# Differential attention: weights times values in three float32r passes for two query tiles at once

## The chip, the cores and the metric

The kernel runs on one core of one Trainium2 chip. The metric is the device time of one launch, in microseconds (us). Before the change three runs gave 2757.2 to 2759.38 us, with a median of 2757.73 us.

The engines are named as the profile names them: PE is TensorE's matrix multiplier, PEld its weight load, DVE is VectorE, ACT is ScalarE, POOL is GpSimd, SP issues the DMAs. A matmul has a *stationary* operand (the weights that are loaded) and a *moving* operand (what streams past it); its result lands in PSUM, which has eight banks of 512 fp32 numbers per partition.

## The reference, cut to what matters

The whole program is a two-layer encoder trunk: 1024 tokens, model width 1024, fp32. Layer 0 mixes tokens with neighbourhood attention, layer 1 with dense differential attention; each layer ends with a gated convolutional feed-forward part and a gated embedding. The change is in layer 1's attention, which has 8 heads, each with two score maps of width 64 and values of width 128:

```python
s = jnp.einsum('bhmqd,bhmkd->bhmqk', qb, k) + bias      # two maps m per head
a = jax.nn.softmax(s, axis=-1)
w = a[:, :, 0] - lam_full * a[:, :, 1]                  # one weight matrix
o = jnp.einsum('bhqk,bhkd->bhqd', w, v)                 # weights times values
o = rms_norm(o, subln_g) * (1.0 - lambda_init)          # norm over the 128 of a head
o = o.transpose(0, 2, 1, 3).reshape(B, S, D) @ w_o
```

## The kernel before, in words

**Order of the work.** The kernel is written in Python on top of a scheduler. TensorE's instructions run in exactly the order in which the program writes them (`manual_schedule` for PE). The order on ACT, DVE, POOL and SP is chosen when the program is compiled, by a planner that walks the program with estimated times; at run time every engine then works through its own list strictly in that order. Waits between engines are put in by the framework, from which part of a buffer each instruction reads or writes. A buffer out of a pool can be handed on only when the last reader of its previous content is done.

**Precision.** A product in fp32 is made in one of two ways. Either the fp32 operands go to a matmul as they are; such a 128x128x128 product shows as two PE instructions in the trace. Or both operands are split into a rounded part and a rest in the type float32r, `hi = round(x)` on ACT (`high`, L135) and `lo = x - hi` on DVE (`low`, L138), and three matmuls are made, hi*hi, hi*lo and lo*hi (`mm3`, L169 to L174).

**The stage of the change** is `da` (L659). It runs over 64 steps n, eight query tiles t of 128 for each of eight heads. For one n:

- `da_scores` (L583): twelve float32r matmuls make the two score maps of 128x1024 in four PSUM banks (pool "s", L598). Then `softmax_pre` per map: on DVE, add the bias and find the minimum (the scores carry a negative sign; L441); on ACT, the exponential with its sum (L445). Then on DVE the reciprocals (L605, L607), the factor (L606), and the combination of both maps into one weight matrix (L608). The row scale `r0` is kept for later.
- `da_turn` (L611), in two halves g: four 128x128 transposes on PE into one PSUM bank (L620), then a copy to `wT`: half 0 on ACT (L623), half 1 on DVE (L625).
- `da_values` (L627): eight fp32 products, with the turned weights `wT` stationary and the values `V` moving (L634). The result has queries on the partitions, so the head's norm is along the free axis: a square with sum on ACT (L637), a small DVE operation (L638), a power on POOL (L184), and the scaling on DVE (L640).
- `da_out` (L643): one transpose of the normed tile on PE (L648), a scaled copy on ACT (L653 or L656), a DMA to `oT` in HBM (L657).

`da` runs these one step apart: in iteration n it calls the values of n-1, the scores of n+1, the two halves of the turn of n, and the output of n-1.

**The stream.** Between them PE works on something else: `qkv_stream` (L296), a generator that makes the keys, queries and values of the *next* head, eight accumulating three-matmul steps per 512 columns. `tick(part)` (L403) takes `6 * part` steps from it. After a block the keys and queries are split out of PSUM (L135 with L138, L145 with L146); the values are copied (L382), turned by four transposes per half (`transposed`, L203), and copied on ACT to `v` (L372). `wblock` (L288) loads and splits the next weights. Near the end the stream goes on with the embeddings (`embeddings`, L1432) and the first rows of the output product (`first_out`, L782); their weights are split by `jobs`, one of which each call of `job` (L739) takes from a list and places behind two given instructions.

**PSUM.** The eight banks are four for the scores, two for the stream (pool "pj") and two in the pool "tr", which serves `bank()`: the values' result, the halves of the turn and the turned values. The values' bank is held from `da_values` to the copy in `da_out`, which reads it.

Of the kernel before, what the change touches and what calls it, by code (L numbers as in the profile page):

```python
# [16 lines left out]
P = 128  # L17
# [74 lines left out]
class Trunk:  # L92
# [203 lines left out]
    def qkv_stream(self, layer, hT, x, first, mid):  # L296
# [7 lines left out]
        for j in range(KT):  # L304
            A = self.page(self.r2, "r2", (P, 4, SEQ), F32R)
# [56 lines left out]
            if layer == 0:  # L362
                v = B[:, 2:4].rearrange("p a (t m w) -> p (a t) m w", t=4, m=2)

                def put(g, t):
                    o, t = v[:, 4 * g : 4 * g + 4], t.rearrange("p k (m w) -> p k m w", m=2)
                    self.split(t, o[:, :, :, 0:64], o[:, :, :, 64:128])
            else:
                v = self.page(x, "v", (P, KT, P))

                def put(g, t):
                    nc.scalar.activation(v[:, 4 * g : 4 * g + 4], t, AF.Copy)  # L372
# [64 lines left out]
    def softmax_pre(self, s, bias, e):  # L437

        nc = self.nc
        mn = self.col("mn")  # L440
        nc.vector.tensor_tensor_reduce(  # L441
            out=e, in0=s, in1=bias, scale=1.0, scalar=3e38, op0=ALU.add, op1=ALU.min, accum_out=mn
        )
        sm = self.col("sum")
        self.exp = nc.scalar.activation(e, e, AF.Exp, bias=mn, scale=-1.0, accum_out=sm).ins  # L445
        return sm
# [136 lines left out]
    def da_scores(self, x, n):  # L583
# [17 lines left out]
        r0, sm = [self.softmax_pre(s[m], self.T[:, a : a + SEQ], e[m]) for m in range(2)]  # L601
        w = e[0]
        self.chunk[n] = w, r0
# [7 lines left out]
    def da_turn(self, x, n, g):  # L611
        nc = self.nc
        w, r0 = self.chunk[n][:2]
        if g == 0:
            self.chunk[n] = w, r0, self.page(x, "wT", (P, KT, P))
        wT = self.chunk[n][2]
        t = self.bank()
        for k in range(4):
            c = (4 * g + k) * P
            nc.tensor.transpose(t[:, k * P : k * P + P], w[:, c : c + P], self.ident)  # L620
        t = t.rearrange("p (k t) -> p k t", k=4)
        if g == 0:
            self.turned_w = nc.scalar.activation(wT[:, 0:4], t, AF.Copy).ins  # L623
        else:
            self.job(self.turned_w, nc.vector.tensor_copy(wT[:, 4:8], t).ins)  # L625

    def da_values(self, x, n):  # L627
        nc = self.nc
        V = self.v[2 * (n // NT)]
        _, r0, wT = self.chunk[n]  # L630
        b = self.bank()
        o = b[:, :P]
        for k in range(KT):
            nc.tensor.matmul(o, wT[:, k], V[:, k], start=k == 0, stop=k == KT - 1)  # L634
        os = self.page(x, "os", (P, P))
        r = self.col("ss")
        nc.scalar.activation(os, o, AF.Square, scale=r0, accum_out=r)  # L637
        nc.vector.tensor_scalar(out=r, in0=r, scalar1=1.0 / P, scalar2=EPS, op0=ALU.mult, op1=ALU.add)  # L638
        self.root(r)
        nc.vector.tensor_scalar(out=os, in0=o, scalar1=r0, scalar2=r, op0=ALU.mult, op1=ALU.mult)  # L640
        self.chunk[n] = b, os

    def da_out(self, x, n, oT):  # L643
        nc = self.nc
        h, t = n // NT, n % NT
        b, os = self.chunk.pop(n)
        tr = b[:, P : 2 * P]
        nc.tensor.transpose(tr, os, self.ident)  # L648
        cols = slice(t * P, t * P + P)
        if h == D_HEADS - 1:  # L650
            if t == 0:
                self.opage = self.page(self.raw, "raw")
            nc.scalar.activation(self.opage[:, cols], tr, AF.Copy, scale=self.subg)  # L653
        else:
            ot = self.page(x, "ot", (P, P))
            nc.scalar.activation(ot, tr, AF.Copy, scale=self.subg)  # L656
            nc.sync.dma_start(oT[h][:, cols], ot)  # L657

    def da(self, hT, oT, first, mid):  # L659

        N = NT * D_HEADS
        with self.tc.tile_pool(name="xa1", bufs=2, reuse_waits="tile") as x, \
             self.psum("s", 2) as self.ps:
            self.begin(self.qkv_stream(1, hT, x, first, mid))
            self.chunk = {}
            self.need(self.qk, 0)
            self.tick(6 / 6)
            self.da_scores(x, 0)
            self.tick(6 / 6)
# [762 lines left out]
    def embeddings(self, layer):  # L1432

        nc = self.nc
        a = self.page(self.r2, "r2", (P, 2, 2, SEQ), F32R)
        b = self.page(self.r2, "r2", (P, 2, 2, D), F32R)
        load = []
        for k in range(2):
            rows = slice(k * P, k * P + P)
            for o, src in ((a, self.i["pT"]), (b, self.i["ple_w_proj"])):  # L1440
# [4 lines left out]
        else:  # L1445
# [16 lines left out]
            self.jobs += [job] * 4  # L1462
# [141 lines left out]
```

## Time and profile before

| | |
|---|---|
| median of three runs | 2757.73 us |
| the profiled execution's own time | 2757.19 us |
| its span, first to last instruction | 2755.4 us |
| mean granted TensorE clock | 0.994 |
| PE busy over the span | 98% |
| DVE, ACT, POOL busy over the span | 70%, 48%, 17% |
| the stage `da`, by the starts of its instructions | about 1348 to 1928 us |

Between the span and the execution's own time lie 1.8 us that the profile does not divide up. PE's ends are modelled, so that neighbouring matmuls overlap in the rows; what counts is the distance from one start to the next. A row of a timeline gives the start in us, the busy time in us, the engine, the line, the operation, the buffers, the shape and the count.

### The profile page before, as it was taken

The page shows a single profiled execution, that of the slowest core. Times are in us where ns is not written, and L with a number is a line of the kernel's source. Part 1 is how long each engine was busy: PE and PEld are TensorE (multiplying, and loading weights), DVE is VectorE, ACT ScalarE, POOL GpSimd, SP SyncE. Part 2 cuts the span into 40 slices and gives each one's busy share as a digit, 9 for nine tenths or more (in the row PEclk, how much of TensorE's full clock was granted, in tenths as well). Part 3 has the DMA queues.
Part 4 walks back from the last instruction along what each step waited for, and adds up shares of the span by engine and source line. Part 5 has one row for each costly group of instructions (what it writes and reads, how often), then busy time and mean ns, then how long its engine had stood idle before and what let it go on. Part 6 is the DMA issues. An engine that isn't in the chain of part 4 may idle for free.

```text
span 2755.4 us, 36831 instructions
## 1 busy us (share of the span) xinstructions
PE 2695.6 (98%) x13568; PEld 2229.1 (81%) x13568; DVE 1939.4 (70%) x3317; ACT 1320.1 (48%) x2467; POOL 463.2 (17%) x461
## 2 busy tenths in 40 slices
PE   7999998999999999999999999999999999999998
PEld 5888887877888888888788888887887888888887
DVE  5677777579777777676566666676688777776664
ACT  4555556354443445454355555555454434444452
POOL 2121120004333310001000000000105343300000
PEclk9999999999999999999999999999999999999999
DMA  6412214533332374343211111123413323372343
GB/s 183 172 53 68 63 52 151 147 92 110 113 105 90 115 263 129 101 151 109 99 46 46 45 46 46 54 77 120 141 61 122 115 92 115 97 285 96 115 143 106
DMA packets 129477, 298.49 MB, mean 108 GB/s; under 512 B 11753, under 2 KB 37737, under 8 KB 129297
## 3 DMA queue, kind: packets, MB, share of 16 engines
q1 hardware_dynamic: 129296, 296.15, 32.7%
q8 instruction: 106, 1.74, 0.3%
q14 instruction: 75, 0.61, 0.1%
HBM read 221.69 MB, written 86.61 MB: 112 GB/s over the span
## 4 chain that ended last, share of the span: by engine, by line
PE 86%; DMA 5%; DVE 5%; ACT 2%; issue 1%; POOL 0%; SPq 0%; ACTq 0%; POOLq 0%; DVEq 0%
PE b L172 20%; PE b L173 20%; PE b L174 20%; PE g L762 6%; PE m L762 5%; PE b L634 4%; PE s L598 3%; PE b L620 2%; PE b L203 2%; PE av L506 2%; PE b L488 1%; DMA r<-in_ffn_w_out 1%; PE b L762 1%; DMA raw<-in_qkv 1%; DMA x<-in_x 1%
## 5 line engine op out<-in xcount | busy, mean ns | idle before, releaser
L172 PE MATMUL b<-r,ws 128*128 128x512 f32 (+1 forms) x1328 | 550.1, 414 | 6.9 <-DVE u L1120 4.4
L173 PE MATMUL b<-r,ws 128*128 128x512 f32 (+1 forms) x1328 | 519.4, 391 | 1.0 <-DVE r L138 1.0
L174 PE MATMUL b<-r,ws 128*128 128x512 f32 (+1 forms) x1328 | 519.2, 391 | 0.5 <-DVE ws L138 0.5
L172 PEld LDWEIGHTS b<-r,ws 128*128 128x128 f32 x1328 | 253.0, 191 | 56.3 <-DVE u L1120 5.7
L174 PEld LDWEIGHTS b<-r,ws 128*128 128x128 f32 x1328 | 251.9, 190 | 54.7 <-DVE ws L138 1.0
L173 PEld LDWEIGHTS b<-r,ws 128*128 128x128 f32 x1328 | 253.7, 191 | 38.3 <-DVE r L138 3.1
L172 PE MATMUL b<-r,r 128*128 128x512 f32 x680 | 269.2, 396 | 8.5 <-ACT r L135 5.1
L184 POOL TENSOR_TENSOR ss<-ss,mhalf 128x1 f32<-128x1 f32 x136 | 84.3, 620 | 1136.8 <-DVE ss L638 564.5
L445 ACT ACTIVATE E<-E,mn 128x1024 f32<-128x1024 f32 (+2 forms) x256 | 221.4, 866 | 111.9 <-DVE mn L441 111.7
L172 PE MATMUL b<-r,wa 128*128 128x512 f32 x688 | 268.1, 390 | 3.2 <-DVE B L1132 2.9
L174 PE MATMUL b<-r,wa 128*128 128x512 f32 x688 | 268.0, 389 | 0.0
L173 PE MATMUL b<-r,wa 128*128 128x512 f32 x688 | 267.7, 389 | 0.0
L174 PE MATMUL b<-r,r 128*128 128x512 f32 x680 | 265.3, 390 | 1.0 <-DVE r L138 1.0
L173 PE MATMUL b<-r,r 128*128 128x512 f32 x680 | 265.7, 391 | 0.5 <-DVE r L138 0.5
L138 DVE TENSOR_TENSOR ws<-raw,ws 128x512 fp32r<-128x512 f32 (+3 forms) x168 | 171.7, 1029 | 59.8 <-ACT ws L135 57.2
L138 DVE TENSOR_TENSOR r<-raw,r 128x512 fp32r<-128x512 f32 (+1 forms) x170 | 129.1, 766 | 112.7 <-ACT r L135 109.6
L135 ACT ACTIVATE r<-raw 128x512 fp32r<-128x512 f32 (+1 forms) x170 | 112.4, 669 | 193.3 <-PE b L173 160.3
L135 ACT ACTIVATE ws<-raw 128x512 fp32r<-128x512 f32 (+3 forms) x168 | 124.2, 748 | 131.7 <-PE b L174 52.3
L172 PEld LDWEIGHTS b<-r,r 128*128 128x128 f32 x680 | 128.0, 188 | 37.4 <-ACT r L135 5.3
L762 PE MATMUL m<-r,ws 128*128 128x512 f32 x672 | 155.9, 391 | 0.0
L762 PE MATMUL g<-r,ws 128*128 128x512 f32 x672 | 155.8, 391 | 0.0
L172 PEld LDWEIGHTS b<-r,wa 128*128 128x128 f32 x688 | 129.1, 188 | 31.4 <-DVE B L1132 4.2
(178 smaller groups left out, 5144.1 us busy)
## 6 DMA issues: line engine op xcount, KB each, us to landing
raw<-in_w_in SPq DMA_DIRECT2D x86, 512.0 KB, 3.5
raw<-in_qkv SPq DMA_DIRECT2D x48, 512.0 KB, 5.6
spillS<-r SPq DMA_DIRECT2D x88, 256.0 KB, 3.2
r<-in_ffn_w_out SPq DMA_DIRECT2D x40, 512.0 KB, 10.5
raw<-spillS SPq DMA_DIRECT2D x40, 512.0 KB, 3.5
spillA<-B SPq DMA_DIRECT2D x66, 256.0 KB, 3.0
raw<-spillA SPq DMA_DIRECT2D x30, 512.0 KB, 3.9
x<-x SPq DMA_DIRECT2D x24, 512.0 KB, 3.5
```

Source lines behind the costliest of these rows:

```text
L135: return self.nc.scalar.activation(hi, src, AF.Copy).ins
L138: return self.nc.vector.tensor_tensor(out=lo, in0=src, in1=hi.bitcast(F32), op=ALU.subtract).ins
L172: mm(out, sta[0], mov[0], start=first, stop=False, skip_group_check=onto)
L173: mm(out, sta[0], mov[1], start=False, stop=False, skip_group_check=onto)
L174: mm(out, sta[1], mov[0], start=False, stop=last, skip_group_check=onto)
L184: self.nc.gpsimd.tensor_tensor(out=ss, in0=ss, in1=self.mhalf, op=ALU.pow)
L203: self.nc.tensor.transpose(t[:, k * P : k * P + P], h[:, c : c + P], self.ident)
L445: self.exp = nc.scalar.activation(e, e, AF.Exp, bias=mn, scale=-1.0, accum_out=sm).ins
L506: nc.tensor.matmul(out, V[:, kb, m], a[:, at * P : (at + w) * P], start=i + z == 0, stop=i == len(steps) - 1 and z == 1)
L598: nc.tensor.matmul(s[m][:, w], A[o, a, q], A[o, b, w], start=z == 0, stop=z == 2)
L634: nc.tensor.matmul(o, wT[:, k], V[:, k], start=k == 0, stop=k == KT - 1)
L762: mm(out[half], a, b[:, w], start=first and k + z == 0, stop=last and k == n - 1 and z == 2)
```

## The change

`da_values` now serves two query tiles at once, after every second tile. The roles are swapped: the values are stationary, split into hi and lo, and the turned weights of both tiles, also split, are the moving operand, 256 wide; each of the eight key blocks takes three matmuls (`mm3`). The result has the value's width on the partitions, so it is copied out on ACT and turned back by two transposes (`da_norm`) before the norm, and turned once more by `da_out`. Both halves of `da_turn` are now split (ACT and DVE) rather than copied, and so are the turned values. `wT` is one fixed buffer for a pair; it takes one of the four "r2" pages, and the heads' keys and queries go round the other three. The embeddings' operands move into those pages, their loads come in another order, and two of their four jobs are held back until the page they write is free. The ticks between the parts are new: half a tile's steps (0.5) between the halves of a turn, then 0.3 after an even-numbered tile and 0.7 after an odd-numbered one, ahead of the values.

```diff
@@ qkv_stream
-            A = self.page(self.r2, "r2", (P, 4, SEQ), F32R)
+            A = self.page(self.r2, "r2", (P, 4, SEQ), F32R) if layer == 0 else self.pages[j % 3]
...
-                v = self.page(x, "v", (P, KT, P))
+                v = self.page(x, "v", (P, 2, KT, P), F32R)
 
                 def put(g, t):
-                    nc.scalar.activation(v[:, 4 * g : 4 * g + 4], t, AF.Copy)
+                    self.split(t, v[:, 0, 4 * g : 4 * g + 4], v[:, 1, 4 * g : 4 * g + 4])
@@ da_turn
+        w, u = self.chunk[n], n % 2
         t = self.bank()
         for k in range(4):
             c = (4 * g + k) * P
-            nc.tensor.transpose(t[:, k * P : k * P + P], w[:, c : c + P], self.ident)
-        t = t.rearrange("p (k t) -> p k t", k=4)
-        if g == 0:
-            self.turned_w = nc.scalar.activation(wT[:, 0:4], t, AF.Copy).ins
-        else:
-            self.job(self.turned_w, nc.vector.tensor_copy(wT[:, 4:8], t).ins)
+            self.nc.tensor.transpose(t[:, k * P : k * P + P], w[:, c : c + P], self.ident)
+        did = self.split(t.rearrange("p (k t) -> p k t", k=4), *(a[:, 4 * g : 4 * g + 4, u] for a in self.wT))
+        if g == 1:
+            self.job(*did)
@@ da_values
-        o = b[:, :P]
+        o, (hi, lo) = b[:, : 2 * P], self.wT
         for k in range(KT):
-            nc.tensor.matmul(o, wT[:, k], V[:, k], start=k == 0, stop=k == KT - 1)
-        os = self.page(x, "os", (P, P))
...
+            self.mm3(
+                o, (V[:, 0, k], V[:, 1, k]), [a[:, k].rearrange("p u t -> p (u t)") for a in (hi, lo)], k == 0, k == KT - 1
+            )
+        os = self.page(x, "os", (P, 2, P), bufs=1)
+        self.nc.scalar.activation(os.rearrange("p u t -> p (u t)"), o, AF.Copy)
+        self.pair = b.rearrange("p (z u t) -> p z u t", z=2, u=2), os
+
+    def da_norm(self, x, n):
...
+        b, os = self.pair
+        r0 = self.sums.pop(0)
+        for u in range(2):
+            nc.tensor.transpose(b[:, 1, u], os[:, u], self.ident)
+        for u in range(2):
+            o, q, r = b[:, 1, u], r0[:, u : u + 1], self.col("ss")
+            nc.scalar.activation(os[:, u], o, AF.Square, scale=q, accum_out=r)
+            nc.vector.tensor_scalar(out=r, in0=r, scalar1=1.0 / P, scalar2=EPS, op0=ALU.mult, op1=ALU.add)
+            self.root(r)
+            nc.vector.tensor_scalar(out=os[:, u], in0=o, scalar1=q, scalar2=r, op0=ALU.mult, op1=ALU.mult)
@@ da_out
-        nc.tensor.transpose(tr, os, self.ident)
+        for u in range(2):
+            nc.tensor.transpose(b[:, 0, u], os[:, u], self.ident)
...
+        nc.scalar.activation(out, b[:, 0].rearrange("p u t -> p (u t)"), AF.Copy, scale=self.subg)
+        if h < D_HEADS - 1:
+            nc.sync.dma_start(oT[h][:, cols], out)
@@ da
+            self.pages = [self.page(self.r2, "r2", (P, 4, SEQ), F32R) for _ in range(4)]
+            w = self.pages[3].rearrange("p a n -> p (a n)").rearrange("p (z k u t) -> p z k u t", z=2, k=KT, u=2)
+            self.wT = w[:, 0], w[:, 1]
...
             for n in range(N + 1):
-                if n > 0:
+                if n % 2 == 0 and n > 0:
                     self.need(self.v, (n - 1) // NT * 2 + 1)
                     self.da_values(x, n - 1)
                 if n + 1 < N:
                     self.need(self.qk, (n + 1) // NT)
                     self.da_scores(x, n + 1)
+                if n + 1 >= N - NT - 1:
+                    self.jobs += self.after_keys
+                    self.after_keys.clear()
+                if n % 2 == 0 and n > 0:
+                    self.da_norm(x, n - 1)
+                elif n > 1:
+                    self.da_out(x, n - 2, oT)
                 if n < N:
                     self.da_turn(x, n, 0)
-                self.tick(0.34)
-                if n < N:
+                    self.tick(0.5)
                     self.da_turn(x, n, 1)
-                self.tick(0.16)
-                if n > 0:
-                    self.da_out(x, n - 1, oT)
-                self.tick(0.5)
+                    self.tick(0.7 if n % 2 else 0.3)
             self.drain()
+            self.da_out(x, N - 1, oT)
@@ embeddings
+            a, b = (self.pages[k].rearrange("p (k z) n -> p k z n", k=2) for k in (2, 0))
...
-            self.jobs += [job] * 4
+            self.jobs += [job] * 2
+            self.after_keys += [job] * 2
```

More of the change, by code (lines that the diff above doesn't have):

```diff
@@ L600, in da_scores @@
         e = [self.page(x, f"E{m}") for m in range(2)]
-        r0, sm = [self.softmax_pre(s[m], self.T[:, a : a + SEQ], e[m]) for m in range(2)]
-        w = e[0]
-        self.chunk[n] = w, r0
+        if n % 2 == 0:
+            self.sums.append(self.page(x, "r0", (P, 2)))
+        r0 = self.sums[-1][:, n % 2 : n % 2 + 1]
+        bias = self.T[:, a : a + SEQ]
+        self.softmax_pre(s[0], bias, e[0], r0)
+        sm = self.softmax_pre(s[1], bias, e[1])
+        w = self.chunk[n] = e[0]
         c = self.col("c")
@@ new lines, in da_turn @@
+        did = self.split(t.rearrange("p (k t) -> p k t", k=4), *(a[:, 4 * g : 4 * g + 4, u] for a in self.wT))
+        if g == 1:
+            self.job(*did)
+    def da_values(self, x, n):
+        V = self.v[2 * (n // NT)]
+        b = self.bank()
+        o, (hi, lo) = b[:, : 2 * P], self.wT
+        for k in range(KT):
+            self.mm3(
[4 more added lines that the diff above has]
+        self.pair = b.rearrange("p (z u t) -> p z u t", z=2, u=2), os
```

48 lines of the change are left out of this document (15 added, 33 removed).

## The prediction, made before the changed kernel had run

> **What bounds the kernel now.** I read the page first, then the stage in a table of windows, then PE's timeline, then DVE and ACT beside it.
>
> ```profile
> span 2755.4 us, 36831 instructions
> PE 2695.6 (98%) x13568; PEld 2229.1 (81%) x13568; DVE 1939.4 (70%) x3317; ACT 1320.1 (48%) x2467; POOL 463.2 (17%) x461
> ...
> PE 86%; DMA 5%; DVE 5%; ACT 2%; issue 1%; POOL 0%; SPq 0%; ACTq 0%; POOLq 0%; DVEq 0%
> ```
>
> ```profile
> 1435.00:1505.00 70.00, 70.00 (x448) 57.80 (x447) 47.09 (x96) 36.54 (x75) 4.40 (x8) 1.00 0.14 44
> ```
>
> PE carries 86% of the chain. In the second fence (length of the stretch, then PE, PEld, DVE, ACT, POOL busy, then the granted clock) one head of the stage fills PE without a gap at clock 1.00, with DVE busy 67% and ACT 52%. So a PE instruction removed here shortens the kernel, as long as DVE and ACT still keep up. One period, in PE's starts:
>
> ```profile
> 1444.15 1.95 PE L634 MATMUL b<-v,wT 128*128 128x128 f32 x16
> 1446.03 1.66 PE L598 MATMUL s<-r 64*128 64x512 f32 x12
> 1447.62 0.65 PE L620 MATMUL b<-ident,E 128*128 128x128 f32 x4
> 1449.50 0.60 PE L620 MATMUL b<-ident,E 128*128 128x128 f32 x4
> 1450.64 0.27 PE L648 MATMUL b<-ident,os 128*128 128x128 f32 x1
> 1452.82 1.95 PE L634 MATMUL b<-v,wT 128*128 128x128 f32 x16
> ```
>
> ```profile
> 1521.70 0.40 PE L172 MATMUL b<-r,ws 128*128 128x512 f32 x1
> ...
> 1522.39 0.39 PE L172 MATMUL b<-r,ws 128*128 128x512 f32 x1
> ```
>
> Start to start: values 1.88, scores 1.59, first half-turn to second 1.88, second to output 1.14, output to values 2.18; together 8.67 us a tile. A stream step is 0.69 (second fence). By the loop the three stretches hold 2, 1 and 3 steps, which leaves 0.50 and 0.45 for the half-turns and 0.11 for one transpose.
>
> **The change part by part.**
>
> *Values.* The new matmuls have 128x256 moving operands and weights that change as in `mm3`. The trace has that very form in the first projection:
>
> ```profile
> 18.14 0.41 PE L172 MATMUL b<-r,ws 128*128 128x256 f32 x1
> ...
> 20.06 0.41 PE L172 MATMUL b<-r,ws 128*128 128x256 f32 x1
> ...
> 24.09 0.28 PE L172 MATMUL b<-r,ws 128*128 128x256 f32 x1
> ...
> 26.49 0.28 PE L174 MATMUL b<-r,ws 128*128 128x256 f32 x1
> ```
>
> From 24.09 to 26.49 are 20 starts: 0.120 each. (From 18.14 to 20.06, while PE has just begun, nine starts: 0.213.) The stage runs at clock 1.00, so I take 0.120: 24 x 0.120 = 2.88 a pair, where two tiles cost 3.76. That saves 0.88.
>
> The Trainium skill ("TensorE: Matmul & The Clock Gate", Part 3, "The mechanism") speaks against this: a weight load overlaps running matmuls only if it goes to another row group. Here each load fills all rows, so load and stream would add up, and 24 loads would cost more than the page's count of instructions suggests. The rows at 0.120 do not agree: each holds a whole load.
>
> *Transposes.* One a tile (0.22 a pair) becomes two in the norm and two in the output, 4 x 0.11 = 0.44: +0.22.
>
> PE's work per pair falls by 0.66, from 17.34 to 16.68; 32 pairs: **-21.1 us**.
>
> *At the very end* there is no next score to cover the norm:
>
> ```profile
> PE b L648 <- DVE os L640: 1.9, 1, 1.9
> ```
>
> Afterwards the last norm waits only for the copy out of PSUM (about 0.2 handover and 0.4 copy, see below), and the stream's last steps cover the rest: 1.9 - 0.7 = **-1.2 us**.
>
> *DVE and ACT.* The copies become splits:
>
> ```profile
> L625 DVE COPY wT<-b 128x512 f32<-128x512 f32 x62 | 42.5, 685 | 3.0 <-PE b L620 3.0
> ...
> L138 DVE TENSOR_TENSOR r<-b,r 128x512 fp32r<-128x512 f32 x14 | 9.6, 687 | 0.9 <-ACT r L135 0.4
> ```
>
> A rest taken from PSUM costs DVE what the copy did, 0.69, but there are two a tile, and two a head for the values: per head 8 x 0.69 + 2 x 0.69 = 6.9 us more, (47.1 + 6.9) of some 67 us, or 80%. ACT gains 8 x 0.6. Neither is the bound by its sum. What matters is when. One tile before, with DVE and ACT in order of time:
>
> ```profile
> 1446.68 0.15 DVE L638 TENSOR_SCALAR ss<-ss 128x1 f32<-128x1 f32 x1 [1.45 <-ACT os L637]
> 1447.57 0.41 DVE L640 TENSOR_SCALAR os<-b,sum,ss 128x128 f32<-128x128 f32 x1 [0.73 <-POOL ss L184]
> 1447.89 1.21 DVE L441 CUSTOM_DVE_ANT_0 E<-s,T 128x1024 f32<-128x1024 f32 x1
> ...
> 1449.03 1.22 DVE L441 CUSTOM_DVE_ANT_0 E<-s,T 128x1024 f32<-128x1024 f32 x1
> ...
> 1450.18 0.68 DVE L625 COPY wT<-b 128x512 f32<-128x512 f32 x1
> 1451.63 0.17 DVE L605 RECIPROCAL c<-sum 128x1 f32<-128x1 f32 x1 [0.77 <-ACT E L445]
> ...
> 1452.17 1.27 DVE L608 SCALAR_TENSOR_TENSOR E<-E,c,E 128x1024 f32<-128x1024 f32 x1
> ```
>
> ```profile
> 1446.19 0.37 ACT L637 ACTIVATE os<-b,sum 128x128 f32<-128x128 f32 x1 [2.54 <-PE b L634]
> 1446.46 0.19 ACT L637 ACTIVATION_READ_ACCUMULATOR os<-b,sum 128x1 f32 x1
> 1448.31 0.60 ACT L623 ACTIVATE wT<-b 128x512 f32<-128x512 f32 x1 [1.66 <-PE b L620]
> 1449.21 1.15 ACT L445 ACTIVATE E<-E,mn 128x1024 f32<-128x1024 f32 x1 [0.30 <-DVE mn L441]
> ...
> 1450.36 1.15 ACT L445 ACTIVATE E<-E,mn 128x1024 f32<-128x1024 f32 x1
> ```
>
> Measured from the end of the scores (1447.62) the weights are ready at 1452.17 + 1.27, that is 5.8 us later, and PE turns them at 8.67: 2.9 us to spare.
>
> After the change the pair is lopsided. Per pair the ticks come to 3 steps and 1.8 (even tile), 3 and 4.2 (odd tile); carried fractions, which fall just short of a whole in floating point, make them 3 and 2, then 3 and 4. After the scores called in an *even* iteration PE has: two transposes 0.2, first half-turn and 3 steps 2.57, second half-turn and 2 steps 1.83, the next scores 1.59, two transposes 0.2: **6.4 us** until these weights are turned. After those of an odd iteration it is 10.6.
>
> In the even window ACT now has both squares ahead of the first exponential. They are ready 0.45 after the scores (transposes 0.2, handover 0.2 as from 1447.62 + 0.50 to 1448.31) and take 0.45 each (1446.19 to the end of its accumulator row); the split's high part follows, 1.35 to 1.95; then the exponentials from 1.85 rather than 1.59. The weights come at 6.1, so they still fit, with 0.3 spare.
>
> The *spare PSUM bank* does not. The values' bank is held through the whole even iteration, so both half-turns share the other one, and the second waits for the rest of the first. Before, that was ACT's copy alone. Now it is a DVE operation, ready at 1.96 while the second L441 pass (the scores' rows end 0.07 after the next start; with 0.1 of handover, and no L640 ahead of it as at 1447.57, the first pass begins at 0.17, and passes start 1.14 apart) holds DVE until 2.45. If it goes straight after, the bank is free at 2.45 + 0.62 + 0.1 = 3.2; behind the two L638, at 3.6. PE wants it at 2.77. So the stall is 0 (the rest planned between the passes) to 0.8; I take 0.4, as a rest lies nearest to the copy L625, which follows the second pass directly: 32 x 0.4 = **+12.8 us**. Behind that half-turn in PE's order are the steps and the next scores, all late with it.
>
> Once in each of seven heads the first turn of the stream's values falls at the end of an even window and needs the same bank, at about 5.0. The rest of the second half-turn is ready at 4.8, just as L608 is: ahead of it, the bank is free at 5.5; behind it, at 6.7. I take 0.5, bounds 0 and 1.7: 7 x 0.5 = **+3.5 us**.
>
> *Costed at nothing.* The copy of the 256-wide result (0.37 to 0.60 by the ACT rows for 128 and 512) runs under the next scores, 1.59; without them it costs the 0.7 above. The normed tile is ready some 4.5 after the scores, the output wants it at 6.6. The values wait for the odd tile's last rest, up to 6.5 after its scores, and start at 6.0, but only their second four blocks need it, 1.44 later. That waits go by part of a buffer shows here:
>
> ```profile
> 1434.98 0.60 PE L203 MATMUL b<-ident,raw 128*128 128x128 f32 x4
> 1435.42 2.01 PE L634 MATMUL b<-v,wT 128*128 128x128 f32 x16
> ```
>
> ```profile
> 1435.62 0.60 ACT L372 ACTIVATE v<-b 128x512 f32<-128x512 f32 x1 [1.57 <-PE b L203]
> ```
>
> The values start 0.2 before the copy of their second half does. On SP's queue the output stores are half as many and twice as large, a tile later; the next read of them is in the last head. The embeddings' four loads keep their count; the two held back are split by the 57th tile, when the stream wants them. If not, one load and split, 2 to 3 us, would show once.
>
> *Sum:* -21.1 - 1.2 + 12.8 + 3.5 = -6.0, against the profiled execution's 2757.2 (span and 1.8 around it): 2751.2. The median is 0.5 above that execution: **2751.7 us**.
>
> **The rivals.**
>
> *All hidden.* The planner puts the rest of the first half-turn between the passes and its own delays fit into the spare 0.3. For it: DVE is idle a fifth of the time. Against: the high part ends 0.6 after the first pass does. Then 2757.7 - 22.3 = 2735.
>
> *The one bank costs more than the matmuls save (slower).* Place: the second half-turn of every even tile; it decides from 0.66 us a pair, where stall equals saving. Price: 0.8 x 32 = 25.6, the value-turn behind L608 at 1.3 x 7 = 9.1, and where a key or query split lands in the even window (two of four pairs, by the loop) 0.2 x 16 = 3.2: 37.9 - 22.3 = +15.6, 2773 us. For it: two L638 come ready before the rest does. Against: one place in DVE's order undoes half of it.
>
> *The change does not do what it says:* the 256-wide matmuls go at the 0.213 of the early rows, 5.1 us a pair: (5.1 - 3.76 + 0.22) x 32 = +50, 2808 us. Against: the clock was 1.00 and the rows at 0.120 are the same instruction. That is also the way in which the skill's rule on loads would show.
>
> **How the numbers follow.** No change is within 0.2%, 5.5 us. Forecast 0.47 (its own range, with the stall at 0.2 to 0.6 and the value-turn at 0 to 1.0, is 2742 to 2762), all hidden 0.17, one bank 0.31, slow matmuls 0.02, the rest, such as the last head's jobs on a fuller DVE, 0.03 on the slow side. Faster: 0.28 of the forecast's 0.47 and the hidden case, 0.45. Same: 0.15 of it and 0.05 of the bank's, 0.20. Slower: the remaining 0.35. The range 2736 to 2782 leaves out about half of the hidden case and the far end of the bank's.
>
> **What would show it.** The values: 24 matmuls at 0.12, 2.9 us a pair; anything near 0.2 is the third rival. Pair period: 16.7 with all hidden, 17.1 as forecast, above 17.34 slower. PE's waits: the second half-turn on L138's `wT` about 0.4 a time in 32 places, 0 or 0.8 in the rivals; the value-turn on the same. I am wrong if PE waits instead for L608 (the weights late), for the copy of the values' result, or at the values themselves for `wT`; or if DVE in the stage is far from 80% busy.

## The result, and the profile after

The changed kernel is slower. Four runs gave 2787.44 to 2791.79 us, median 2791.27, beside 2758.56 us for the kernel before (four runs, 2757.2 to 2759.66): a ratio of 1.011, 95% interval 1.0097 to 1.0123. The forecast was 2751.7 with a range up to 2782, so the sign and the range were both wrong.

The page of the profiled execution after the change (span; busy time of each engine; the chain that ended last):

```profile
span 2790.0 us, 36344 instructions
PE 2696.6 (97%) x13376; PEld 2214.2 (79%) x13376; DVE 1981.6 (71%) x3397; ACT 1350.4 (48%) x2531; POOL 483.8 (17%) x461
...
PE 28%; DVE 4%; ACT 2%; DMA 1%; issue 1%; POOL 0%; SPq 0%; ACTq 0%; POOLq 0%; DVEq 0%
```

PE is as busy as before (2696.6 against 2695.6) although its last instruction ends later. Modelled ends stretch a busy row wherever PE waits inside it, so busy time is no measure of PE's work here. The chain covers little over a third of the span this time, and no reading below rests on it. The same middle stretch that was quoted before (length, then PE, PEld, DVE, ACT, POOL busy, then the clock):

```profile
1435.00:1505.00 70.00, 66.80 (x411) 53.62 (x412) 49.44 (x97) 37.12 (x77) 5.69 (x7) 1.00 0.13 45
```

PE was busy for 70.00 of 70 us before; now it has holes, at the same clock of 1.00, while DVE is at 71%. How long a head takes is read from the start of its first values matmul to that of the next head. The kernel after, PE's timeline (the first row begins one head, 1517.74 the next):

```profile
1444.63 0.39 PE L172 MATMUL b<-r,v 128*128 128x256 f32 x1 [0.19 <-DVE r L138]
...
1517.74 0.36 PE L172 MATMUL b<-r,v 128*128 128x256 f32 x1
1517.94 0.28 PE L173 MATMUL b<-r,v 128*128 128x256 f32 x1
...
1520.58 0.28 PE L174 MATMUL b<-r,v 128*128 128x256 f32 x1
1520.79 1.65 PE L598 MATMUL s<-r 64*128 64x512 f32 x12
```

The kernel before (its head began at 1435.42, a row that the prediction shows):

```profile
1505.67 0.50 PE L634 MATMUL b<-v,wT 128*128 128x128 f32 x3
```

This head took 70.25 us and takes 73.11. The table splits the stage in this way, by the profiled execution of every kernel of this study. The stage runs from the start of the first scores to the start of the last output transposes. A "middle head" is the mean of the first six distances between heads; "the ends" is what is left: the lead-in, the seventh distance and the last head. The runs were made at several times, and the median of the kernel before, run beside each, moved by up to 3.3 us; so between experiments the ratios say more than differences of medians.

| kernel | time, us | ratio to before | stage | middle head | the ends |
|---|---|---|---|---|---|
| before | 2758.6 to 2761.9, the medians beside each | 1 | 580.0 | 70.25 | 158.5 |
| after | 2791.3 | 1.0110 | 614.3 | 73.26 | 174.8 |
| e1 squares first | 2778.6 | 1.0070 | 602.5 | 73.30 | 162.7 |
| e2 four steps | 2793.1 | 1.0124 | 614.5 | 73.75 | 172.0 |
| e3 both | 2780.3 | 1.0076 | 601.3 | 73.18 | 162.2 |
| e4 4, 3, 3, 2 | 2790.5 | 1.0112 | 617.1 | 73.27 | 177.5 |
| e5 value-turn moved | 2771.6 | 1.0037 | 597.5 | 72.35 | 163.4 |
| e6 ACT frees the bank | 2795.2 | 1.0125 | 620.9 | 75.88 | 165.6 |
| e7 rests on POOL | 2781.1 | 1.0072 | 602.4 | 72.98 | 164.5 |
| e8 no rests | 2750.8 | 0.9963 | 575.4 | 70.27 | 153.8 |
| e9 e5 with 4, 2, 3, 3 | 2770.6 | 1.0037 | 592.2 | 71.83 | 161.2 |
| e10 e9, weights on POOL | 2760.2 | 0.9998 | 582.7 | 70.44 | 160.1 |
| e11 before, weights on POOL | 2761.3 | 0.9998 | 578.4 | 70.26 | 156.8 |
| e12 e5, weights on POOL | 2769.5 | 1.0031 | 591.9 | 71.91 | 160.4 |

The stage grew by 34.3 us and the span by 34.6, so nearly the whole loss lies in this stage: 6 x 3.01 = 18.0 in the middle heads and 16.3 at the ends.

**What PE waits for.** Waits of the stage after the change (engine and buffer, line, what came last, its line; then us in total, times, longest). A wait at the head of a group of transposes shows partly on PE and partly on its weight load, PEld:

```profile
PEld b L621 <- DVE r L138: 22.5, 33, 1.3
PE b L658 <- DVE os L651: 22.3, 17, 4.8
PEld b L203 <- DVE r L138: 11.4, 7, 2.6
PE b L621 <- DVE r L138: 8.7, 33, 0.9
PE b L203 <- DVE r L138: 8.4, 7, 2.2
```

Before, no wait of PE in this stage came to more than 2.6 us in all. Three places have appeared: the output transposes (L658) wait for the scaled tile of the norm (L651); the second half-turn (L621) waits for the rest of the first, 33 times; the first turn of the stream's values (L203) waits for a rest, once in each of seven heads.

*The norm is a chain in which DVE stands twice.* One even window, right after the scores of 1520.79; PE, then DVE, then ACT, then POOL:

```profile
1522.64 0.60 PE L621 MATMUL b<-ident,E 128*128 128x128 f32 x4
1525.57 0.66 PE L621 MATMUL b<-ident,E 128*128 128x128 f32 x4 [0.25 <-DVE r L138]
...
1529.43 0.44 PE L658 MATMUL b<-ident,os 128*128 128x128 f32 x2 [0.23 <-DVE os L651]
```

```profile
1523.62 1.22 DVE L441 CUSTOM_DVE_ANT_0 E<-s,T 128x1024 f32<-128x1024 f32 x1
...
1524.83 0.68 DVE L138 TENSOR_TENSOR r<-b,r 128x512 fp32r<-128x512 f32 x1
1525.64 0.41 DVE L651 TENSOR_SCALAR os<-b,r,ss 128x128 f32<-128x128 f32 x1
...
1527.19 1.27 DVE L612 SCALAR_TENSOR_TENSOR E<-E,c,E 128x1024 f32<-128x1024 f32 x1
...
1528.97 0.40 DVE L651 TENSOR_SCALAR os<-b,r,ss 128x128 f32<-128x128 f32 x1
```

```profile
1522.93 0.37 ACT L648 ACTIVATE os<-b,r 128x128 f32<-128x128 f32 x1 [1.65 <-PE b L645]
...
1526.52 0.36 ACT L648 ACTIVATE os<-b,r 128x128 f32<-128x128 f32 x1
```

```profile
1490.05 0.55 POOL L184 TENSOR_TENSOR ss<-ss,mhalf 128x1 f32<-128x1 f32 x1 [2.65 <-DVE c L610]
...
1527.30 1.56 POOL L184 TENSOR_TENSOR ss<-ss,mhalf 128x1 f32<-128x1 f32 x1 [1.69 <-DVE ss L649]
```

The rest (1524.83) goes straight after the second L441 pass, and the second half-turn starts at 1525.57, 2.93 after the first; with nothing in the way a half-turn takes 0.36 and three steps 2.16, so it is 0.41 late. The first tile's square runs at 1522.93, the second's only at 1526.52, after the scaling of the first (1525.64), as `da_norm` is written; in all 32 pairs it comes after that scaling's end. That it waits, and is not merely planned late, shows in the very last pair, where ACT has nothing else to do and the scaling ends at 1959.93:

```profile
1959.97 0.37 ACT L648 ACTIVATE os<-b,r 128x128 f32<-128x128 f32 x1 [1.36 <-DVE os L651]
```

From the second square on, the second tile still needs L649, the power on POOL and L651, and in the ordinary window the last of them starts at 1528.97, 6.6 after the scores' end (1520.79 + 1.58 = 1522.37). The output comes at 1529.43.

*In the third pair of each head DVE and ACT are full.* DVE, then ACT, then PE, in the even window whose scores end 0.1 before the first row:

```profile
1484.27 1.23 DVE L441 CUSTOM_DVE_ANT_0 E<-s,T 128x1024 f32<-128x1024 f32 x1 [4.23 <-PE s L598]
...
1487.79 1.23 DVE L138 TENSOR_TENSOR ws<-raw,ws 128x1024 fp32r<-128x1024 f32 x1
1488.93 0.68 DVE L146 SCALAR_TENSOR_TENSOR r<-b,r 128x512 fp32r<-128x512 f32 x1
...
1490.15 1.27 DVE L612 SCALAR_TENSOR_TENSOR E<-E,c,E 128x1024 f32<-128x1024 f32 x1
```

```profile
1486.71 1.04 ACT L135 ACTIVATE ws<-raw 128x1024 fp32r<-128x1024 f32 x1
...
1488.14 1.15 ACT L445 ACTIVATE E<-E,mn 128x1024 f32<-128x1024 f32 x1
```

```profile
1492.39 0.44 PE L658 MATMUL b<-ident,os 128*128 128x128 f32 x2 [1.39 <-DVE os L651]
```

A weight block's rest (1487.79) and a query split (1488.93) lie in the window as well. DVE has hardly a moment free from 1484.27 on, the weights are combined only at 1490.15 + 1.27, that is 7.25 after the scores, the scaling comes behind them at 1491.93, and PE waits 1.39. ACT is no earlier: the same block's rounding (1486.71) and the query's (0.58) stand between the two exponentials. The second one ends at 1489.29, and its sum is read out until 1489.37; the reciprocal on DVE (L609), which needs it, starts at 1489.54. So a DVE with nothing else to do could not have begun the combination much before it did here.

*In the last head the embeddings' jobs stand in front.* DVE, then PE:

```profile
1898.57 0.15 DVE L649 TENSOR_SCALAR ss<-ss 128x1 f32<-128x1 f32 x1
...
1899.23 1.21 DVE L138 TENSOR_TENSOR r<-r,r 128x1024 fp32r<-128x1024 f32 x1
1900.37 1.22 DVE L441 CUSTOM_DVE_ANT_0 E<-s,T 128x1024 f32<-128x1024 f32 x1
...
1902.65 0.41 DVE L651 TENSOR_SCALAR os<-b,r,ss 128x128 f32<-128x128 f32 x1
```

```profile
1903.12 0.69 PE L658 MATMUL b<-ident,os 128*128 128x128 f32 x2 [4.85 <-DVE os L651]
```

Between L649 and the scaling DVE's list holds rests, the job's among them, and two passes of L441. The power on POOL was done at 1899.41. PE stands for 4.85 us, and for 4.71 and 2.46 in the next two even windows: 12.0 in all, beside 16.3 lost at the ends.

Each of the three waits also slows what follows it. Right behind the first, from 1903.20 to 1906.60, the granted clock is 0.51, and the stream's matmuls start 0.43 apart (1904.88, 1905.31, 1905.74) in place of 0.23. The stage has 13.6 us at clock 0.5 in this kernel, 6.8 before and 3.4 in e1 below. What such a stretch costs can be estimated from pairs of tiles that differ in nothing else: the fourth pair of a head in e3 took 21.22 with one and 19.66 without, the third in e2 20.32 and 18.75, so about 1.6.

### The profile page after: what moved, and what is told of

Its sections match the earlier page's. It is cut to its first block, busy times and chain, and to the rows that moved or that the text cites. A ratio compares the mean times of both kernels' runs of the same rounds, so it can differ in the third digit from the quotient of the medians.

```text
span 2790.0 us, 36344 instructions
## 1 busy us (share of the span) xinstructions
PE 2696.6 (97%) x13376; PEld 2214.2 (79%) x13376; DVE 1981.6 (71%) x3397; ACT 1350.4 (48%) x2531; POOL 483.8 (17%) x461
## 5 line engine op out<-in xcount | busy, mean ns | idle before, releaser
L184 POOL TENSOR_TENSOR ss<-ss,mhalf 128x1 f32<-128x1 f32 x136 | 104.8, 772 | 1151.8 <-DVE ss L649 558.2
L441 DVE CUSTOM_DVE_ANT_0 E<-s,T 128x1024 f32<-128x1024 f32 x128 | 151.4, 1220 | 114.3 <-PE s L598 114.3
## 6 DMA issues: line engine op xcount, KB each, us to landing
r<-in_ffn_w_out SPq DMA_DIRECT2D x40, 512.0 KB, 10.2
```

Source lines behind the costliest of these rows:

```text
L184: self.nc.gpsimd.tensor_tensor(out=ss, in0=ss, in1=self.mhalf, op=ALU.pow)
L441: nc.vector.tensor_tensor_reduce(out=e, in0=s, in1=bias, scale=1.0, scalar=3e38, op0=ALU.add, op1=ALU.min, accum_out=mn)
```

## The experiments

In all diffs the steps are sixths of a `tick`; the change's order is 3 and 2 after the first and second half-turn of the even tile, 3 and 4 of the odd tile, written 3, 2, 3, 4. Where the order is changed (e2, e3, e4, e9, e10), the loop also starts from `tick(8.25 / 6)` in place of `tick(8 / 6)`, so that sixths carried over do not fall short of a whole step.

**e1, both squares before the first scaling.**

```diff
+        rs = [self.col("ss") for u in range(2)]
         for u in range(2):
-            o, q, r = b[:, 1, u], r0[:, u : u + 1], self.col("ss")
-            nc.scalar.activation(os[:, u], o, AF.Square, scale=q, accum_out=r)
+            nc.scalar.activation(os[:, u], b[:, 1, u], AF.Square, scale=r0[:, u : u + 1], accum_out=rs[u])
+        for u in range(2):
+            o, q, r = b[:, 1, u], r0[:, u : u + 1], rs[u]
```

> Only the order in da_norm changes: both squares are written ahead of the first tile's scaling, so that the second square no longer follows the scaling, which reads the same PSUM bank. Theory A (the output transposes wait because the program's order makes the second tile's norm a serial chain behind the first one's): the second square follows the first directly, PE's waits of the output transposes on the scaling fall from 22 us to under 3, and the time falls by 18 to 23 us, to about 2770. Rival B (DVE is simply too full in the even windows): the waits move elsewhere and the time stays within 6 us of 2791. Rival C (the planner puts the exponentials ahead of the second square anyway): order and time unchanged.

Measured: 2778.62 us, ratio 1.007 (1.0055 to 1.0085), 12.7 less than after. The output's wait for the scaling is gone from the list of waits, yet the gain is not its 22.3. The table shows where it lies: the ends fell by 12.1, the middle heads stayed at 73.3. In the third pair, PE's timeline, and the waits that now lead the list:

```profile
1489.58 0.44 PE L660 MATMUL b<-ident,os 128*128 128x128 f32 x2
1491.01 0.63 PE L621 MATMUL b<-ident,E 128*128 128x128 f32 x4 [0.99 <-DVE E L612]
```

```profile
PE b L203 <- DVE r L138: 10.2, 7, 2.4
PE b L621 <- DVE E L612: 7.4, 7, 1.4
```

The output goes at once now, and the half-turn behind it waits 0.99 for the weights (L612), which the same full DVE delivers late. So the norm's order cost 12 us in the last head (75.1 before the edit, 63.4 with it), where the stretches at half clock went with the waits; in the middle heads its wait only stood in front of another.

**e2 and e3, four steps before the second half-turn of the even tile (4, 1, 3, 4), without and with e1's edit.**

```diff
-                    self.tick(0.5)
+                    self.tick((4, 3)[n % 2] / 6)
                     self.da_turn(x, n, 1)
-                    self.tick(0.7 if n % 2 else 0.3)
+                    self.tick((1, 4)[n % 2] / 6)
```

> The changed kernel with the steps after the four half-turns of a pair as 4, 1, 3, 4 instead of 3, 2, 3, 4, nothing else. Theory A: the second half-turn of an even tile no longer waits for its bank (8.7 us of recorded PE waits, about 13 us of PE time, gone), but the next scores then come 0.4 earlier while the norm's chain is as long as before, so the output transposes wait more in about half the pairs: 4 to 9 us faster, about 2785. Rival B (DVE full): no change within 3 us. If the waits of the half-turn were all that matters: 13 us faster, 2778.

> Both edits. Theory A: the gains add, since the output transposes no longer wait: 2791 - 20 - 13 = about 2758, level with the kernel before; what is left of the loss is the turned values' wait (8 us of records) and the last head. Rival B: within 8 us of 2791.

Measured: 2793.07 (1.0124, 1.0109 to 1.0139) and 2780.33 us (1.0076, 1.0061 to 1.0091): no gain on after or on e1. The 0.4 at the half-turn did go in most places, but the steps taken from later in the window left nothing to cover what comes next: the value-turn's total rose from 10.2 in e1 to 14.0 in e3. In e3 that longer wait was followed by half clock in two of the six middle heads, which took 74.2 us; the other four took 72.6 to 72.8, against 73.1 to 73.7 in e1. So this order gives back about 0.6 of the 1.6 us a head that the half-turns cost, and the clock takes it again.

**e4, steps 4, 3, 3, 2, with e1's edit.**

```diff
-                    self.tick(0.7 if n % 2 else 0.3)
+                    self.tick((3, 2)[n % 2] / 6)
```

> Squares first, and the steps as 4, 3, 3, 2: two steps more in the even window, two fewer between the odd tile's second half-turn and the values. Theory A: the even window is 2 x 0.69 longer, so neither half-turn nor output nor the turned values wait there; the values' last four blocks need the odd tile's last rest 1.4 us after they start, which is about when it comes: 2738 to 2752, faster than before by 0.2 to 0.7%. If the values then wait for that rest at their start (whole buffer): 0.5 to 1.5 us a pair more, 2760 to 2790. Rival B: no faster than the third kernel.

Measured: 2790.5 us, 1.0112 (1.0095 to 1.0128), 12 worse than e1 where a large gain was expected. The even windows were freed, and the values, with two steps ahead of them instead of four, waited for the odd tile's last rest, about 1.6 us a head; with a longer wait at the value-turn (1.84 against 1.30) the middle head came out level. The 12 us lie at the ends. The seventh distance took 82.1 us against 75.8 in e1: in its last pair PE waited 1.76 for that rest, 2.95 and 1.41 at the value-turn and 2.37 for a copy of the embeddings' result out of PSUM on ACT, with three stretches at half clock.

**e5, the first value-turn moved to the fourth step of the next head's keys, with e1's edit.**

```diff
                 for kt, _ in enumerate(self.proj(wk, hT, ps, tb, a)):
+                    if layer == 1 and tb == 0 and kt == 3:
+                        values((0,))
```

> Squares first, and the first turn of the stream's values is moved from the end of the even window (where it wants the bank that the second half-turn's rest still holds) into the next odd window, four steps into the next head's keys. Theory A (the one spare bank): the value-turn's waits, 10 us of records and 1.35 us a head in PE's starts, shrink to a third: 6 to 9 us faster than squares first alone, about 2771. Rival B (DVE full; the wait belongs to DVE's backlog and goes where the turn goes): no faster than 2778.

Measured: 2771.58 us, 1.0037 (1.0024 to 1.005), 7 less than e1. The value-turn's wait fell from 10.2 to

```profile
PE b L203 <- DVE r L138: 3.8, 7, 1.8
```

and the middle head from 73.30 to 72.35: here a wait went that had none behind it.

**e6, ACT copies the even tile's first half-turn out of PSUM, and the split works from the copy, with e1's edit.**

```diff
+        if u == 0 and g == 0:
+            self.nc.scalar.activation(xw, t, AF.Copy)
+            t = xw
+        did = self.split(t, hi, lo)
```

> Squares first, and for the first half-turn of every even tile ACT copies the bank out to SBUF and the split is made from that copy (one ACT operation more, 0.5 us, the rest stays on DVE). Theory A: the bank no longer waits for DVE, so the second half-turn's wait (0.47 a pair, 15 us) is gone, but ACT's extra 0.5 us delays the exponentials of the same window, so the weights come later and half of it returns: 4 to 12 us faster than squares first alone, 2766 to 2775. Rival B: DVE's list is unchanged, so the time is too: 2778.

Measured: 2795.23 us, 1.0125 (1.011 to 1.014), 17 worse than e1. The even tile's bank came free without DVE, but the split starts only after the copy, and the wait was paid at the value-turn, for the weights (L613, 13.4 us), and at half-turns behind the rests that are still on DVE (10.8 us in 17 places):

```profile
PE b L203 <- DVE r L138: 17.5, 7, 3.5
```

**e7, ACT copies all half-turns out and POOL makes all their rests, with e1's edit.**

```diff
+        self.nc.scalar.activation(xw, t, AF.Copy)
+        did = self.high(xw, hi), self.nc.gpsimd.tensor_tensor(out=lo, in0=xw, in1=hi.bitcast(F32), op=ALU.subtract).ins
```

> Squares first, and every half-turn is copied out by ACT, rounded from the copy by ACT, and its rest taken by POOL from SBUF (1.4 us each there by the rows of the feed-forward part); DVE loses all rests of the weights. Theory A: banks come free by ACT alone and DVE is emptier than in the kernel before: 2742 to 2762, if ACT (some 75% busy) does not become the bound. Rival D (POOL's operations and DVE's slow each other, as POOL's power taking 1.5 instead of 0.55 us beside L612 suggests): DVE's softmax passes lengthen and the time is 2775 or more.

Measured: 2781.13 us, 1.0072 (1.0057 to 1.0087), level with e1. Now the values wait for POOL, and the half-turns for the weights (L613, 11.0 us in 15 places), with two operations of ACT for each half-turn in place of one:

```profile
PE b L173 <- POOL r L627: 9.2, 10, 1.8
```

**e8, no rests of the turned weights, with e1's edit.** The second of the three passes reads the rounded weights again, so PE's work is the same.

```diff
-        did = self.split(t.rearrange("p (k t) -> p k t", k=4), *(a[:, 4 * g : 4 * g + 4, u] for a in self.wT))
+        hi = self.wT[0][:, 4 * g : 4 * g + 4, u]
+        did = self.high(t, hi), self.exp
```

> Squares first with the rests of the weights left out: DVE makes none, and the second of the three passes reads the rounded part again, so PE does the same work (the output is then less exact). This takes away 128 x 4 / 4 = 128 DVE operations of 0.69 us and nothing else. Theory A: half-turns wait only for ACT; what is left are the waits of the value-turns: 2738 to 2752, faster than the kernel before, and the difference to squares first (2778) is what the rests cost, 26 to 40 us. Rival E (the waits come from the lopsided windows and the longer chain to the weights, not from the rests): 2765 or more.

Measured: 2750.8 us, 0.9963 (0.9948 to 0.9977), 28 less than e1 and faster than before. The first values matmul of the second, third and fourth pair of a head, PE's timeline:

```profile
1453.83 0.28 PE L172 MATMUL b<-r,v 128*128 128x256 f32 x1
...
1470.66 0.28 PE L172 MATMUL b<-r,v 128*128 128x256 f32 x1
...
1488.72 0.28 PE L172 MATMUL b<-r,v 128*128 128x256 f32 x1
```

A pair without a wait takes 16.83 us, where two tiles took 17.34: this is PE's real saving, 0.51. The third pair still takes 18.06, with the block and the query still to be split; its half-turn waits 1.04 for the weights, and one in the fourth pair 0.47 for a rest of the stream's values. So the middle head, 70.27, is only level with the kernel before: those waits use up the four times 0.51 that PE saves, and what the stage gains over before, 4.6 us, lies at the ends. (The profiled execution of e8 is 8.9 us shorter than that of before; another 4.2 of it lie ahead of the stage, where the two kernels do the same.) The 128 rests of 0.69 us thus cost 28 us of a stage in which DVE is busy for no more than 71% of the time.

**e9, e12 and e10: the step order, DVE's load, and both.** e9 is e5 with the steps 4, 2, 3, 3. e12 is e5 with the rests of this stage's streamed weight blocks on POOL instead of DVE. e10 has both.

```diff
+        self.high(raw, hi)
+        self.nc.gpsimd.tensor_tensor(out=lo, in0=raw, in1=hi.bitcast(F32), op=ALU.subtract)
...
-            wv = self.wblock(W[2 * KT + j])
+            wv = self.wblock(W[2 * KT + j], layer == 1)
```

> Squares first, the first value-turn moved, and the steps as 4, 2, 3, 3: one step more between the half-turns of an even tile, one fewer between the odd tile's second half-turn and the values. Theory A2 (the loss is the rests' time on DVE inside a window that PE leaves too short; it shows at whichever instruction of that window wants the bank next): the even window is 0.69 longer than in the run before, which covers the half-turn's 0.47 in every pair and half of the 1.15 in the third pair of a head, and three steps still cover the values' rest: about 2 us a head and 16 us in all, 2752 to 2760, level with the kernel before. If a longer window only moves the wait to the values, as with the steps 4, 3, 3, 2: 2768 or more.

> The same, and the rests of the stream's weight blocks of this stage (three a head, 1.22 us each on DVE, SBUF to SBUF) are taken by POOL. Theory A2: DVE loses 3.7 us a head, most of it in or next to even windows, so the wait in the third pair of a head goes as well: 2745 to 2755, slightly faster than the kernel before. Rival D (POOL work slows DVE, or the norm's power queues behind a POOL operation of some 2.8 us and the output transposes wait for it): no faster than the run beside it, or slower.

> The kernel with the squares first, the value-turn moved and the weight rests on POOL, but with the change's own order of steps (3, 2, 3, 4 sixths) instead of 4, 2, 3, 3. Theory (DVE's room decides, and where the steps stand matters little): 2758 to 2763, as with 4, 2, 3, 3 (2760.2). Rival (a longer first step removes the half-turn's wait as soon as DVE has room, and only then): the wait of 0.4 a pair is back, 32 x 0.4 = 13 less what POOL's help takes off it, 2766 to 2773.

Measured: e9 2770.59 (1.0037, 1.0024 to 1.005), e12 2769.54 (1.0031, 1.002 to 1.0042), e10 2760.2 us (0.9998, 0.9989 to 1.0007). Each edit alone takes 0.5 and 0.4 off the middle head's 72.35, both take 1.9. The waits of e9, e12 and e10 say why:

```profile
PE b L173 <- DVE r L138: 8.5, 8, 1.4
```

```profile
PE b L633 <- DVE r L138: 19.8, 40, 1.2
```

```profile
PE b L173 <- DVE r L138: 1.4, 1, 1.4
```

With the steps alone (e9), the half-turn's stall is traded for a wait of the values for their last rest, in one pair of each head. With DVE relieved alone (e12), half-turns still wait 40 times, since the rest before them still follows the second pass. Together the rest is on time at both places in three pairs of four. What is left in e10 is mostly the third pair:

```profile
PE b L633 <- DVE r L138: 9.1, 10, 1.1
```

It waits 1.05 in each of six heads. There DVE, without the block's rest, itself stood 0.44 for the second exponential, which ACT delivers late, and the factor (L622) took 0.67 in place of 0.22 beside POOL's work (see the last section). The second theory of e12 was right, and the first, that the order of steps does not matter, fell.

**e11, the kernel before with the weight rests on POOL.**

> The kernel before with this stage's weight-block rests taken by POOL instead of DVE: the same edit that brought 10 us on the changed kernel. Theory (DVE's work costs time only where PE waits for it): before, the two middle windows show PE busy 70.00 of 70 us and no row of PE waiting for r of L138, so nothing is gained: 2756 to 2761, level with before, and PE stays at 70.00. Rival (the edit helps by itself, wherever it is made, for instance in the first and last head): 2748 to 2753, and then the changed kernel would stay behind before on equal terms by the same 10 us.

Measured: 2761.3 us, 0.9998 (0.9989 to 1.0007), and a middle stretch that PE still fills:

```profile
1435.00:1505.00 70.00, 70.00 (x449) 57.73 (x447) 43.76 (x93) 36.44 (x75) 12.52 (x11) 1.00 0.12 42
```

The relief that brought e10 some 10 us brings nothing here, where PE hardly waited for DVE. No version that computes the full product beat the kernel before; the best, e10, is level with it.

## Why the prediction was wrong

**Values: right.** From 1517.94 to 1520.58 lie 22 distances, 0.120 each, and a group of 24 with the step to the scores takes 2.96 (3.05 in the rows shown, right after a value-turn), forecast 2.88. The rule of the Trainium skill that the prediction weighed ("TensorE: Matmul & The Clock Gate", Part 3, "The mechanism") doesn't agree with this trace: loads that fill all rows, 0.19 each, run under matmuls 0.120 apart. The prediction left out that the same section names a second case, a load into the background weight buffer, which fits these rows.

**Transposes: mis-sized.** Forecast +0.22 a pair; all transposes of a pair took 1.60 before (half-turns included) and 1.97 after where nothing waits: +0.37, partly made up in the stream's steps (-0.08). With the 2.96 above, PE's work falls by 0.51 rather than 0.66, -16 us rather than -21.1.

**The half-turn: right.** 0.41 in 32 places is 13 us, as chosen. **The value-turn:** forecast 0.5, measured 1.1 by the starts, within its bounds, 8 us instead of 3.5. **The very end:** right in kind; the wait on the copy was 0.47 where 0.7 was forecast (1957.59). DVE was forecast at 80% of a head and is at 71 to 72%: its busy time a head rose from 47.3 to 52.6, by 5.3 where 6.9 was forecast, and the head is longer than the 67 us of that sum.

**Where it failed: what was costed at nothing.** "The normed tile is ready some 4.5 after the scores, the output wants it at 6.6." In the ordinary window it is ready at 6.6 + 0.4, and in the last head PE stood 4.85 us for it. The sum took both squares to run back to back, which the order as written did not let them do, and it gave the norm's hops no queueing on DVE. The 12 us in the last head (e1) belong to this step; "the last head's jobs on a fuller DVE" stood among the rest with a chance of 0.03.

The second failure is "the weights come at 6.1, so they still fit, with 0.3 spare". In the third pair they come at 7.25, because a weight block and a query are split in the same window, on ACT (1.04 and 0.58) as on DVE (1.23 and 0.68). Both were there before, and the profile of before shows what they do to that tile, whose scores end at 1473.62:

```profile
1476.18 1.22 DVE L138 TENSOR_TENSOR ws<-raw,ws 128x1024 fp32r<-128x1024 f32 x1
...
1477.92 0.68 DVE L146 SCALAR_TENSOR_TENSOR r<-b,r 128x512 fp32r<-128x512 f32 x1
...
1479.17 1.27 DVE L608 SCALAR_TENSOR_TENSOR E<-E,c,E 128x1024 f32<-128x1024 f32 x1
```

Here the weights came 6.8 after the scores, more than the 6.4 that the new even window has, and not 5.8 as in the one tile that the prediction read; the spare was 1.85 and not 2.9. The sum counted the new work in the window and not the old; only the one-bank rival gave such a split a price, 0.2. For a middle head: PE's work -2.0, half-turns +1.6, value-turn +1.1, the waits before the output in the first and third pair +1.75; the sum of +2.45 is short of the measured +3.01 by 0.56 that no single wait accounts for.

Of the rivals, the one bank had the right side and the right kind of cause, a window that DVE can't serve in time, but its 2773 left out the norm and the last head. e8 shows that the rests are the largest part: without them the middle head falls by 3.0 to 70.27. It does not show whether DVE's time or the banks held until a rest is done weighs more; e10, which frees DVE of other work and leaves the banks as they are, wins most of it back in the middle heads, with the value-turn and the steps moved. e9, e10 and e12 show that no single place is the cause.

## What to carry to other kernels

An engine that is 70% busy can set the pace if its work falls due in windows: list everything it has to do between two deadlines, the old work with the new, before counting on slack, in the fullest of the repeats and not in one that happens to be read, and do the same for the engine that feeds it. A wait's total in a list is not what its removal brings; ask which wait stands behind it on the same engine, as e1 showed in the middle heads and e3 and e6 at the value-turn. And when work is moved off the busiest engine onto one that was hidden, both the place of its consumer and the room on the new engine may have to change before anything is gained.

## What the runs showed of the hardware

**POOL's power was held up by DVE.** It takes 0.55 us alone. At 1527.30 it began after L612 (1527.19) and ended at 1528.86, 0.40 after L612 did; at 1490.05 it began 0.10 ahead of L612 (1490.15) and took its 0.55. The stage's group of it, before and after:

```profile
L184 POOL TENSOR_TENSOR ss<-ss,mhalf 128x1 f32<-128x1 f32 x64 | 36.0, 563 | 564.5 <-DVE ss L638 564.5
```

```profile
L184 POOL TENSOR_TENSOR ss<-ss,mhalf 128x1 f32<-128x1 f32 x64 | 56.7, 886 | 574.0 <-DVE ss L649 558.2 <-DVE c L610 15.9
```

The Trainium skill ("SBUF — State Buffer", "Who interferes with whom") says that a DVE instruction with two SBUF inputs and a GpSimd instruction that reads SBUF shut each other out, and that the one issued first wins. With DVE first this trace agrees: all 22 powers that began behind L612 took 1.51 to 1.58, the other 42 took 0.55. With POOL first the short power held nothing up that the rows show, as L612 took its 1.27 at 1490.15 too. A longer one did: in e10 POOL's rest of a weight block ran from 1485.93 to 1488.34, and L622, begun at 1487.69, ended at 1488.36; it took 0.66 to 0.67 in six such places and 0.22 elsewhere.

**Reads of one PSUM bank by ACT and DVE went one after the other.** The second square reads the bank that the first tile's scaling reads, and came after it; in the last pair ACT stood idle for it (1959.97, above). The Trainium skill ("PSUM — Partial Sum Buffer", "PSUM bank collisions raise a hardware error") says that accesses of two engines to the same bank and partitions must be kept apart, reads too. With the order of e1 the two squares follow each other directly, 0.36 apart. Whether the shared bank or something else in the order as written held the second one was not tried by itself.

**A long wait of PE cost more than itself.** In the stages of all fourteen kernels, each of the eleven waits of PE of 2.9 us or more went with a stretch of 3.4 or 6.8 us at clock 0.5. Of those between 1.7 and 2.7 some did: in e3 two of the six value-turns that waited 1.84 or 1.83, the others not. Shorter ones did not by themselves; in e5 a stretch followed two waits of 0.99 and 1.27 that lay 2 us apart.
